# Sliding-window attention on one square of keys per head: own and older scores merged by a mask, values by differences

## The chip, the cores and the metric

The kernel runs on one core of a Trainium2 chip. A core has TensorE (PE: matmuls, and a separate stream of weight loads, PEld), VectorE (DVE), ScalarE (ACT), GpSimd (POOL) and SyncE (SP), which issues most of the transfers. The metric is the device time of one execution in microseconds (us); lower is better.

## The reference

One inference step of a trunk of two layers on 1024 prompt tokens and 8 single new tokens, in float32, with a width of 1024. Layer 0 is a gated linear recurrence with its MLP, layer 1 is sliding-window attention with its MLP. The change touches the attention of the prompt tokens only. There are 16 query heads, 4 key heads and 64 elements per head; the window is 128 tokens, and blocks are as long as the window.

```python
def sink_attention(q, k, v, dist, mask, sinks):
    s = jnp.einsum('...qkgd,...skd->...kgqs', q, k) * (HEAD_DIM ** -0.5)
    s = s - alibi_slopes()[:, :, None, None] * dist
    s = jnp.where(mask, s, NEG_INF)
    sink = sinks.reshape(N_KV, GROUP)[:, :, None, None]
    m = jnp.maximum(jnp.max(s, axis=-1, keepdims=True), sink)
    e = jnp.exp(s - m)
    p = e / (jnp.sum(e, axis=-1, keepdims=True) + jnp.exp(sink - m))
    return jnp.einsum('...kgqs,...skd->...qkgd', p, v)

def swa_prompt(...):                       # per block of 128 queries: keys of the block before and of its own
    ...
    dist = qi + BLOCK - si                 # qi: 0..127, si: 0..255
    mask = (dist >= 0) & (dist < WINDOW) & (key_pos >= 0)
    o = sink_attention(qb, with_prev(k), with_prev(v), dist, mask[:, None, None], sinks)
```

For a query `qi` of a block the window holds the own block's keys 0 to `qi` and the block before's keys `qi`+1 to 127. That is 128 keys of the 256: for each column of 128, either the own or the older key is inside the window, and never both.

## The kernel before, in words

The attention stage is one interleaved stream. It has 64 steps, `STEPS[j] = (t, b)`: `t` is one of 8 pairs of heads, `b` one of 8 blocks of 128 queries. Each step has three parts, and different steps' parts overlap by an order written out by hand (lines 1133 to 1175):

- `stage_a(j)` runs three steps ahead of the others (`AHEAD = 3`). For each of the two heads GpSimd makes the bias from the distances (line 953) and copies the sink's score into the last column of the probabilities' tile `se` (line 955). TensorE makes the scores of 128 queries by 256 keys, with the keys in a high and a low part (line 959), in one of two PSUM banks called "S". VectorE adds scores and bias and takes the row's extreme (line 963), ScalarE takes the exponential and its sum (line 966), VectorE the reciprocal (line 968), and GpSimd multiplies by it (line 971). Block 0 has no block before it and uses 128 keys.
- `stage_b(j)` transposes the probabilities on TensorE, four squares of 128 by 128 (two heads, two blocks of keys; two squares where b is 0), into the only PSUM bank "T" (line 981). One copy takes them to the tile `pt` in SBUF, by VectorE at even and by ScalarE at odd steps (line 986).
- `stage_c`, after every four steps, multiplies with the values (line 1003) into bank "O" and copies the result out (lines 1008 to 1013).

Between these parts TensorE does work that doesn't depend on them, called `fill`. Until step 52 (`J0`) this is the projection of the later queries and keys, 3 groups of three matmuls per step (line 886). From then on it is the output projection (line 245), whose weights are called `wo1`. Weights arrive as `raw`, ScalarE casts them to a high part `wh` (line 185), and VectorE makes the low part `wl` (line 186). The tuple `WHEN` says at which step each of the first output weights is fetched and split. Weights, values, probabilities and transposed probabilities share one pool of 12 working tiles, `W`; another pool is `A`.

Names in the rows: `bS`, `bT`, `bO`, `bP` are the PSUM banks of scores, transposes, value products and projections; `se` the probabilities, `den` their row sums, `fac` factors per token, `con` constants (distances, identity), `hh` and `hl` the high and low part of the layer's input.

Of the kernel before, what the change touches and what calls it, by code (L numbers as in the profile page):

```python
# [10 lines left out]
F32 = mybir.dt.float32  # L11
F32R = mybir.dt.float32r
AF = mybir.ActivationFunctionType
ALU = mybir.AluOpType
# [36 lines left out]
    VEC[_n] = (_off, _w)  # L51
    _off += _w
NVEC = _off
C_DIST, C_ID, C_BLK = 0, 256, 384
NCONST = 512

# [6 lines left out]
def trunk(ctx: ExitStack, tc: tile.TileContext, I, O):  # L65
# [37 lines left out]
    def W(s="w"):  # L103
        return wp.tile([P, T], F32, tag="W", name=nm(s))
# [29 lines left out]
        return c if isinstance(c, slice) else slice(c * CH, (c + 1) * CH)  # L134


    con = cp.tile([P, NCONST], F32, name="con")
    ones = cp.tile([P, P], F32, name="ones")
    pool.memset(ones, 1.0 / D)
    vec = cp.tile([P, NVEC], F32, name="vec")  # L140
# [1 line left out]
    act.dma_start(vec, I["vec"])  # L142
    ident = con[:, C_ID:C_ID + P]
    blk = con[:, C_BLK:C_BLK + P]
    distM = con[:, C_DIST:C_DIST + 256]

    def V(n, m=0):
        o, _ = VEC[n]
# [43 lines left out]
    def add_units(name, src, n, alloc=lambda j: W):  # L192
        for j in range(n):
            units.append((name, j, src[j], alloc(j)))
# [8 lines left out]
    for layer in range(2):  # L203
        add_units(f"up{layer}", I["w_up"][layer], 2 * NPAIR, lambda j: None)
        for b in range(4 * NCK):
            for j in range(2):
                units.append((f"dn{layer}", 2 * b + j, I[f"w_dn{layer}"][2 * b + j][:, 0:2 * P * len(CHUNKS[layer][b // 4])], None))
        add_units(f"ds{layer}", I[f"w_dn{layer}"][8 * NCK:], 2 * (NPAIR - NSP[layer]), lambda j: W)
        if layer == 0:
            for n, t in (("k", 0), ("q", 0), ("v", 0), ("v", 1), ("q", 1), ("q", 2), ("q", 3), ("k", 1),  # L210
                         ("q", 4), ("q", 5), ("q", 6), ("q", 7)):
                units.append((n, t, I["w_qkv"][{"q": 0, "k": 8, "v": 10}[n] + t], W))
            add_units("wo1", I["w_out1"], 8, lambda j: A if j in (2, 4) else W)
    index = {(n, j): k for k, (n, j, _, _) in enumerate(units)}
    nloaded = [0]

# [529 lines left out]
    def attention(hs):  # L746
# [141 lines left out]
                    yield  # L888
                due[2].append(lambda c=c, sx=take(c, o): evac(c, sx))

        v_tiles = [W("v") for _ in range(2)]
        vnew = tc.dram_tile([2, D], F32, name="vnew")

        def v_proj():
            w = [unit("v", 0, 1), unit("v", 1, 1)]

            def mms(o, sl):
                n = 0
                for k in range(M8):
                    wh, wl = w[k // 4]  # L900
                    xh, xl = hs[k]
                    ws = slice((k % 4) * 256, (k % 4) * 256 + 256)
                    for xt, wt in ((xh, wh), (xh, wl), (xl, wh)):
                        pe.matmul(o, lhsT=r_(xt[:, sl]), rhs=r_(wt[:, ws]), start=(n == 0), stop=(n == 3 * M8 - 1))  # L904
                        n += 1

            for b2 in range(NB // 2):
                ps = B("S")
                for j in range(2):
                    b = 2 * b2 + j  # L910
                    mms(ps[:, j * 256:j * 256 + 256], slice(b * P, b * P + P))
                for p, copy in enumerate((act.copy, dve.tensor_copy)):
                    copy(v_tiles[p][:, 2 * b2 * P:2 * b2 * P + 2 * P].rearrange("p (b d) -> p b d", b=2),
                         ps.rearrange("p (b q d) -> p b q d", b=2, q=2)[:, :, p, :])
                if b2 > 1:
                    stats0.pop()()
                if b2 == 3:
                    vo = S("vo")
                    act.copy(vo[:, :256], ps[:, 256:512])
                    sp.dma_start(O["v"], vo[:, :256])  # L920
            ps = B("T")
            mms(ps[:NS, :256], slice(SEQ, T))
            vo = S("vo")
            act.copy(vo[:NS, :256], ps[:NS, :256])
            sp.dma_start(vnew.rearrange("h (n j) -> (h n) j", n=4), vo[:NS, :256])

        bias2 = A("bias")
        ses = [W("se"), W("se")]
        ses = [x[:, h * 514:h * 514 + 514].rearrange("p (u k) -> p u k", u=2) for x in ses for h in range(2)]
        outs = {}  # L930
        ohl = {}
        srcs = [None] * M8
# [10 lines left out]
        def stage_a(j):  # L943
            t, b = STEPS[j]
            p, i = divmod(t, 4)
            se, dn, s = ses[j % 4], den[j % 4], B("S")
            hd = heads(t)
            k0 = max(b - 1, 0) * P
            n = P if b == 0 else 2 * P
            f = fac[t % 3]  # L950
            for u in range(2):
                o = (j % 2) * 512 + u * 256
                pool.tensor_scalar(bias2[:, o + 256 - n:o + 256], distM[:, 256 - n:256], f[:, 2 * NB + 2 * b + u:2 * NB + 2 * b + u + 1],  # L953
                                   0.25 * SLOPES[hd[u]], ALU.mult, ALU.mult)
            pool.tensor_copy(se[:, :, 256], nsink[:, hd[0]:hd[1] + 1:4])
            for u in range(2):
                for a, y in enumerate(kst[p][u]):
                  with after_values():
                    pe.matmul(s[:, u * 256:u * 256 + 256], lhsT=r_(qs[t][u][:, b * P:b * P + P]), rhs=r_(y[:, k0:k0 + 256]),  # L959
                              start=(a == 0), stop=(a == 1))  # L960
            for u in range(2):
                o = (j % 2) * 512 + u * 256 + 256
                dve.tensor_tensor_reduce(  # L963
                    se[:, u, 256 - n:256], s[:, u * 256:u * 256 + n], bias2[:, o - n:o],
                    scale=f[:, 2 * b + u:2 * b + u + 1], scalar=nsink[:, hd[u]:hd[u] + 1], op0=ALU.add, op1=ALU.min, accum_out=dn[:, u:u + 1])
                act.activation(se[:, u, 256 - n:257], se[:, u, 256 - n:257], AF.Exp, scale=-1.0,  # L966
                               bias=dn[:, u:u + 1], accum_out=dn[:, 2 + u:3 + u])
            dve.reciprocal(dn[:, 2:4], dn[:, 2:4])  # L968
            for u in range(2):
                e = se[:, u, 256 - n:256]  # L970
                pool.tensor_scalar(e, e, dn[:, 2 + u:3 + u], 0.0, ALU.mult, ALU.add)  # L971


        def stage_b(j):
            b = STEPS[j][1]
            se, pt = ses[j % 4], B("T")
            first = 1 if b == 0 else 0
            for h in range(first, 2):
                for u in range(2):
                  with after_values():  # L980
                    pe.transpose(pt[:, h * 256 + u * P:h * 256 + u * P + P], se[:, u, h * P:h * P + P], ident)  # L981
            if j % 2 == 0:
                live["pair"] = W("pt")
            pw = live["pair"][:, j % 2 * 512:j % 2 * 512 + 512]
            d = slice(256 * first, 512)
            (act.copy if j % 2 else dve.tensor_copy)(pw[:, d], pt[:, d])
            live["pt", j] = pw

        def stage_c(k):
            t, b0 = STEPS[4 * k]  # L990
            if b0 == 0 and t < 6:
                outs[t] = A("o")
            elif b0 == 0:
                srcs[t] = ohl[t] = (A("oh"), A("ol"))
            op, chain = B("O"), last["mm"]
            for b in range(b0 + 3, b0 - 1, -1):
                pw = live.pop(("pt", 4 * k + b - b0))
                first = 1 if b == 0 else 0
                for h in range(first, 2):
                    for u in range(2):  # L1000
                        at = (b - 1 + h) * P + 64 * u
                        with tc.issue_after(chain):
                            chain = pe.matmul(op[64 * u:64 * u + 64, (b - b0) * P:(b - b0) * P + P], lhsT=v_tiles[t // 4][:, at:at + 64],  # L1003
                                              rhs=pw[:, h * 256 + u * P:h * 256 + u * P + P], start=(h == first), stop=(h == 1)).ins
            last["values"] = chain
            dst = slice(b0 * P, b0 * P + 512)
            if t < 6:
                act.copy(outs[t][:, dst][:, 0:256], op[:, 0:256])
                dve.tensor_copy(outs[t][:, dst][:, 256:512], op[:, 256:512])
            else:  # L1010
                oh, ol = [x[:, dst] for x in ohl[t]]
                last["o"] = act.copy(r_(oh), op).ins
                dve.tensor_tensor(r_(ol), op, oh, ALU.subtract)
# [117 lines left out]
                next(fill, None)  # L1131

        NJ = 8 * NB
        WHEN = (44, 47, 49, 54, 60)
        AHEAD, T0, T1, TF, J0, JS = 3, 24, 5, 3.0, 52, 46
        take(T0)
        for j in range(AHEAD):
# [116 lines left out]
        with tc.issue_after(last["mm"]):  # L1254
            token_factors(ssq, rx[:, cs(c)])

    queue(sp, sp.dma_start, con, I["con"])
    cst = cp.tile([P, M8, 3, NS], F32, name="cst")
    pre = aux[:, 2 * P:2 * P + M8 * NS].rearrange("p (m n) -> p m n", m=M8)
    tap = S("tap")[:, :M8 * NS].rearrange("p (m n) -> p m n", m=M8)  # L1260
# [199 lines left out]
def _constants():  # L1460
# [1 line left out]
    qi = np.arange(P)[:, None]  # L1462
    si = np.arange(2 * P)[None, :]
    dist = qi + P - si
    con[:, C_DIST:C_DIST + 256] = np.where((dist >= 0) & (dist < P), dist, MASKED)
    con[:, C_ID:C_ID + P] = np.eye(P)
    h = np.arange(P) // 64
    con[:, C_BLK:C_BLK + P] = (h[:, None] == h[None, :]) / 64.0
# [113 lines left out]
```

## Time and profile before

| | |
|---|---|
| median of 3 runs | 1989.66 us (1988.62 to 1989.97) |
| the profiled execution, its own time | 1990.03 us |
| its span in the profile | 1988.1 us (1.93 us lie around it) |
| TensorE busy | 1980.2 us (100%) |
| VectorE, ScalarE, GpSimd busy | 1386.7, 1050.3, 376.2 us |
| TensorE clock granted | 1.00 |
| attention stage, about 1050 to 1256 us | TensorE 204.0 of 206 us, VectorE 141.3, ScalarE 139.1, GpSimd 137.6 |

The profile is one execution. Its groups give for each line and engine the count, the busy time, the mean duration of one instruction in nanoseconds, and the idle time of the engine just before them with what ended it. Matmuls overlap in the records, so a matmul's own duration is more than it adds to TensorE's time; the distance from start to start is what it adds. The chain of waits follows the execution back from its last instruction.

### The profile page before, as it was taken

To read this page: it belongs to the slowest core of one execution; us is meant where nothing else is said; L and a number is where in the kernel's file an instruction comes from. 1 tells how busy PE (TensorE), PEld (TensorE's weight loads), DVE (VectorE), ACT (ScalarE), POOL (GpSimd) and SP (SyncE) were. 2 spreads that over 40 slices of the span, in tenths; PEclk is the share of its full clock that TensorE was granted. 3 is DMA by queue.
4 is the path that set the end of the run, shared out by engine and by line. 5 is a ranking of instruction groups with operands and counts; after the bars stand their busy time and mean duration, and the time that the engine had idled before them with its cause. 6 is when DMAs were issued, how large, how long until landed. Compare 5 with 4: busy or idle time off the path is not lost.

```text
span 1988.1 us, 39291 instructions
## 1 busy us (share of the span) xinstructions
PE 1980.2 (100%) x15452; PEld 1950.6 (98%) x15452; DVE 1386.7 (70%) x2515; ACT 1050.3 (53%) x2049; POOL 376.2 (19%) x688
## 2 busy tenths in 40 slices
PE   9999999999999999999999999999999999999999
PEld 9999999999999999999999999999999999999999
DVE  7986638867666867767755767588666678776673
ACT  8786436444443655545445767465434346554551
POOL 2230100000001233312005767000000002332220
PEclk9999999999999999999999999999999999999999
DMA  5112322444436688777442324523434446877775
GB/s 173 52 44 64 130 99 72 147 147 139 155 129 223 198 224 228 207 186 198 123 126 70 89 72 148 179 78 124 162 127 155 139 150 202 239 210 187 205 193 132
DMA packets 110857, 294.41 MB, mean 148 GB/s; under 512 B 18488, under 2 KB 43328, under 8 KB 110672
## 3 DMA queue, kind: packets, MB, share of 16 engines
q1 hardware_dynamic: 53712, 125.82, 20.7%
q0 software_dynamic: 29024, 97.85, 19.1%
q10 hardware_dynamic: 27936, 68.23, 9.4%
q8 instruction: 121, 1.98, 0.4%
q14 instruction: 64, 0.52, 0.1%
HBM read 170.97 MB, written 108.19 MB: 140 GB/s over the span
## 4 chain that ended last, share of the span: by engine, by line
PE 96%; DVE 1%; DMA 1%; ACT 1%; issue 1%; POOL 0%; ACTq 0%; SPq 0%; DVEq 0%; POOLq 0%
PE bD L557 61%; PE bP L245 11%; PE bS L245 7%; PE bP L886 4%; PE bO L245 3%; PE bT L245 3%; PE bS L959 1%; PE bO L1003 1%; PE bT L981 1%; PE bS L904 1%; DMA tl<-hsum 1%; DVE tl L431 0%; DVE op L425 0%; PE bN L829 0%; PE bN L773 0%
## 5 line engine op out<-in xcount | busy, mean ns | idle before, releaser
L557 PE MATMUL bD<-op,op 128*128 128x258 f32 x5544 | 678.7, 284 | 0.0
L557 PEld LDWEIGHTS bD<-op,op 128*128 128x128 f32 x5544 | 671.2, 190 | 5.0 <-ACT ho L692 4.5
L557 PE MATMUL bD<-tl,op 128*128 128x258 f32 x4704 | 580.4, 284 | 0.5 <-DVE ho L696 0.3
L557 PEld LDWEIGHTS bD<-tl,op 128*128 128x128 f32 x4704 | 570.7, 189 | 7.6 <-ACT ho L692 5.7
L571 POOL DMA_DIRECT2D tl<-hsum x196 | 113.2, 678 | 940.5 <-ACT op L424 414.9
L425 DVE TENSOR_TENSOR op<-ws,op 128x384 fp32r<-128x384 f32 (+2 forms) x288 | 172.2, 606 | 94.1 <-ACT op L424 94.0
L692 ACT COPY he<-bD 128x516 f32<-128x516 f32 x144 | 84.9, 590 | 275.1 <-PE bD L557 275.0
L424 ACT CAST op<-ws 128x384 fp32r<-128x384 f32 (+2 forms) x288 | 158.5, 555 | 109.5 <-PE bD L557 70.9
L692 ACT COPY ho<-bD 128x516 f32<-128x516 f32 x144 | 84.9, 590 | 192.2 <-PE bD L557 192.1
L431 DVE TENSOR_TENSOR tl<-tl 128x516 fp32r<-128x516 f32 x196 | 129.9, 690 | 76.1 <-ACT tl L430 76.0
L424 ACT CAST op<-raw 128x384 fp32r<-128x384 f32 (+2 forms) x216 | 116.9, 556 | 44.0 <-PE bD L557 19.3
L425 DVE TENSOR_TENSOR op<-raw,op 128x384 fp32r<-128x384 f32 (+2 forms) x216 | 127.6, 604 | 6.4 <-ACT op L424 2.4
L700 DVE TENSOR_TENSOR ho<-bD,ho 128x516 f32<-128x516 f32 x72 | 49.9, 693 | 106.5 <-PE bD L557 106.5
L430 ACT CAST tl<-tl 128x516 fp32r<-128x516 f32 x196 | 116.5, 628 | 7.9 <-DMA tl<-hsum 6.7
L963 DVE CUSTOM_DVE_ANT_0 se<-bS,bias,nsink 128x256 f32<-128x256 f32 (+1 forms) x128 | 63.6, 523 | 21.6 <-PE bS L959 15.2
L186 DVE TENSOR_TENSOR wl<-raw,wh 128x1024 fp32r<-128x1024 f32 (+1 forms) x54 | 63.5, 1184 | 20.2 <-ACT wh L185 12.4
L696 DVE TENSOR_TENSOR ho<-bD,ho 128x516 f32<-128x516 f32 x72 | 49.7, 690 | 39.6 <-ACT ho L692 38.8
L966 ACT ACTIVATE se<-se,den 128x257 f32<-128x257 f32 (+1 forms) x128 | 62.8, 492 | 26.7 <-DVE den L963 21.2
L953 POOL TENSOR_SCALAR bias<-con,fac 128x256 f32<-128x256 f32 (+1 forms) x128 | 63.2, 498 | 34.6 <-DVE den L963 24.1
L971 POOL TENSOR_SCALAR se<-se,den 128x256 f32<-128x256 f32 (+1 forms) x128 | 65.5, 525 | 14.0 <-DVE den L968 9.6
L711 POOL DMA_DIRECT2D spill<-ho x32 | 28.6, 892 | 208.6 <-DVE ho L700 206.6
L886 PE MATMUL bP<-hh,wh 128*128 128x384 f32 (+2 forms) x192 | 67.2, 350 | 0.0
(399 smaller groups left out, 3709.0 us busy)
## 6 DMA issues: line engine op xcount, KB each, us to landing
tl<-hsum POOLq DMA_DIRECT2D x196, 258.0 KB, 6.3
raw<-w_up SPq DMA_DIRECT2D x64, 512.0 KB, 4.4
raw<-w_dn SPq DMA_DIRECT2D x72, 384.0 KB, 6.1
spill<-he POOLq DMA_DIRECT2D x32, 516.0 KB, 9.9
spill<-ho POOLq DMA_DIRECT2D x32, 516.0 KB, 7.0
hsum<-ho ACTq DMA_DIRECT2D x28, 516.0 KB, 2.7
hsum<-he ACTq DMA_DIRECT2D x28, 516.0 KB, 2.7
hsum<-ts ACTq DMA_DIRECT2D x28, 516.0 KB, 3.0
```

The source lines that it names most:

```text
L186: eng.tensor_tensor(r_(lo[:, sl]), raw[:, sl], hi[:, sl], ALU.subtract)
L245: last["mm"] = pe.matmul(o, lhsT=r_(wt[:, col(k):col(k) + P]), rhs=r_(xt[:, cs(c)]), start=(k == 0 and a == 0), stop=(k == nk - 1 and a == ...
L424: act.copy(r_(t[:, 0:n]), src)
L425: dve.tensor_tensor(r_(t[:, n:2 * n]), src, t[:, 0:n], ALU.subtract)
L430: act.copy(r_(hi), lo)
L431: dve.tensor_tensor(r_(lo), lo, hi, ALU.subtract)
L557: ins = pe.matmul(d[:, 512 * b:512 * b + QT], lhsT=r_(wt[:, j * P:j * P + P]), rhs=r_(xt[:, QT * b:QT * b + QT]), start=first and j == 0 a ...
L571: pool.dma_start(t[:, n:2 * n], src)
L692: last["copy"] = act.copy(t, f).ins
L886: last["mm"] = pe.matmul(o, lhsT=r_(wt[:, k * P:k * P + P]), rhs=r_(xt[:, sl]), start=(k == 0 and a == 0), stop=(k == M8 - 1 and a == 2)).ins
L963: dve.tensor_tensor_reduce(se[:, u, 256 - n:256], s[:, u * 256:u * 256 + n], bias2[:, o - n:o], scale=f[:, 2 * b + u:2 * b + u + 1], scala ...
L971: pool.tensor_scalar(e, e, dn[:, 2 + u:3 + u], 0.0, ALU.mult, ALU.add)
```

## The change

With b > 0 the scores of 256 keys are still made in the same bank. Then ScalarE copies the own block's 128 columns of both heads to `se`, and VectorE overwrites, where a constant mask of the pair (query, key) says so, with the older block's score: a predicated copy. Bias, score sum, exponential, sum and normalisation then run on 128 columns instead of 256. One square per head is transposed instead of two; ScalarE copies it out at every step, and VectorE writes a second copy multiplied by the transposed mask, which holds the older keys' part alone.

The values follow from: own·V(b) + older·V(b−1) = (own + older)·V(b) + older·(V(b−1) − V(b)). The differences `dv` are made once, by GpSimd, two instructions of 128 by 896. The value products keep their number and shape, four per step (two where b is 0).

The masks are two more blocks of 256 columns in the constants in DRAM, brought by one more transfer on SP into the second half of the bias tile, whose halves had held biases of 256 keys. Two tiles `dv` are added to the pool `W` and one of the two tiles of `se` goes. The tuple `WHEN` has a sixth entry, 62, and the sixth output weight takes its tile from the other pool, `A`.

```diff
-            add_units("wo1", I["w_out1"], 8, lambda j: A if j in (2, 4) else W)
+            add_units("wo1", I["w_out1"], 8, lambda j: A if j in (2, 4, 5) else W)
...
+            for x in v_tiles:
+                dv.append(W("dv"))
+                pool.tensor_tensor(dv[-1][:, 0:SEQ - P], x[:, 0:SEQ - P], x[:, P:SEQ], ALU.subtract)
...
         bias2 = A("bias")
-        ses = [W("se"), W("se")]
-        ses = [x[:, h * 514:h * 514 + 514].rearrange("p (u k) -> p u k", u=2) for x in ses for h in range(2)]
+        sp.dma_start(bias2[:, 512:1024], I["con"][:, C_OWN:])
+        older, older_t = bias2[:, 512:768].bitcast(mybir.dt.int32), bias2[:, 768:1024]
+        ses = W("se")
+        ses = [ses[:, h * 258:h * 258 + 258].rearrange("p (u k) -> p u k", u=2) for h in range(4)]
...
+            bias = [bias2[:, (j % 2) * 256 + u * P:(j % 2) * 256 + u * P + P] for u in range(2)]
             for u in range(2):
-                o = (j % 2) * 512 + u * 256
-                pool.tensor_scalar(bias2[:, o + 256 - n:o + 256], distM[:, 256 - n:256], f[:, 2 * NB + 2 * b + u:2 * NB + 2 * b + u + 1],
+                pool.tensor_scalar(bias[u], dist if b else dist0, f[:, 2 * NB + 2 * b + u:2 * NB + 2 * b + u + 1],
                                    0.25 * SLOPES[hd[u]], ALU.mult, ALU.mult)
...
+            s = s.rearrange("p (u h k) -> p u h k", u=2, h=2)
+            if b:
+                act.copy(se[:, :, 0:P], s[:, :, 1, :])
+                dve.copy_predicated(se[:, :, 0:P], older.rearrange("p (u k) -> p u k", u=2), s[:, :, 0, :])
             for u in range(2):
-                o = (j % 2) * 512 + u * 256 + 256
+                e = se[:, u, 0:P]
                 dve.tensor_tensor_reduce(
-                    se[:, u, 256 - n:256], s[:, u * 256:u * 256 + n], bias2[:, o - n:o],
+                    e, e if b else s[:, u, 0, :], bias[u],
                     scale=f[:, 2 * b + u:2 * b + u + 1], scalar=nsink[:, hd[u]:hd[u] + 1], op0=ALU.add, op1=ALU.min, accum_out=dn[:, u:u + 1])
-                act.activation(se[:, u, 256 - n:257], se[:, u, 256 - n:257], AF.Exp, scale=-1.0,
-                               bias=dn[:, u:u + 1], accum_out=dn[:, 2 + u:3 + u])
+                act.activation(se[:, u, :], se[:, u, :], AF.Exp, scale=-1.0, bias=dn[:, u:u + 1], accum_out=dn[:, 2 + u:3 + u])
...
-            first = 1 if b == 0 else 0
-            for h in range(first, 2):
-                for u in range(2):
-                  with after_values():
-                    pe.transpose(pt[:, h * 256 + u * P:h * 256 + u * P + P], se[:, u, h * P:h * P + P], ident)
+            for u in range(2):
+                with after_values():
+                    pe.transpose(pt[:, u * P:u * P + P], se[:, u, 0:P], ident)
...
-            d = slice(256 * first, 512)
-            (act.copy if j % 2 else dve.tensor_copy)(pw[:, d], pt[:, d])
+            act.copy(pw[:, 0:256], pt[:, 0:256])
+            if b:
+                dve.tensor_tensor(pw[:, 256:512], pt[:, 0:256], older_t, ALU.mult)
...
-                for h in range(first, 2):
+                for h, vb in enumerate(((v_tiles, b), (dv, b - 1)) if b else ((v_tiles, b),)):
...
-        WHEN = (44, 47, 49, 54, 60)
+        WHEN = (44, 47, 49, 54, 60, 62)
```

The order of the instructions on TensorE, at one step of the second pair of heads. Before:

```order
L959 MATMUL bS_12425<-kl_11388,q_11921 128x256
...
L981 MATMUL bT_12443<-con,se_11337 128x128 x4
L886 MATMUL bP_12390<-hh_10743,wh_12021 128x384
L886 MATMUL bP_12390<-hl_10744,wh_12021 128x384
L886 MATMUL bP_12390<-hh_10743,wl_12022 128x384
...
L959 MATMUL bS_12455<-kh_11385,q_11920 128x256
```

The same place on TensorE after the change:

```order
L963 MATMUL bS_12439<-kl_11388,q_11925 128x256
...
L986 MATMUL bT_12459<-con,se_11337 128x128 x2
L886 MATMUL bP_12403<-hh_10743,wh_12025 128x384
L886 MATMUL bP_12403<-hl_10744,wh_12025 128x384
L886 MATMUL bP_12403<-hh_10743,wl_12026 128x384
...
L963 MATMUL bS_12470<-kh_11385,q_11924 128x256
```

Two transposes are left at the place of four; the projection and the scores around them stand as they did.

The order on VectorE at the same place (`ISA` is the score sum, with the reading of its extreme behind it). Before:

```order
L963 ISA se_11337,den_11327<-bS_12425,bias_11335,nsink,fac_11330 128x256
L963 ISA den_11327 128x1
...
L968 RECIPROCAL den_11327<-den_11327 128x2
L963 ISA se_11337,den_11328<-bS_12455,bias_11335,nsink,fac_11330 128x256
L963 ISA den_11328 128x1
...
L986 COPY pt_12476<-bT_12473 128x256
L968 RECIPROCAL den_11328<-den_11328 128x2
```

VectorE after the change:

```order
L968 COPY_PREDICATED se_11337<-bias_11335,bS_12439 128x2x128
L992 TENSOR_TENSOR pt_12430<-bT_12459,bias_11335 128x256
L971 ISA se_11337,den_11327<-se_11337,bias_11335,nsink,fac_11330 128x128
L971 ISA den_11327 128x1
...
L968 COPY_PREDICATED se_11337<-bias_11335,bS_12470 128x2x128
L971 ISA se_11337,den_11328<-se_11337,bias_11335,nsink,fac_11330 128x128
L971 ISA den_11328 128x1
L975 RECIPROCAL den_11327<-den_11327 128x2
```

The predicated copy stands ahead of the score sums, and the multiplication of the step three back stands between them. Both new instructions wait for ScalarE's copy of the same bank.

The order on ScalarE at the end of the stage, where `wh` is a cast of an output weight and `y`, `sq`, `x` belong to the output projection. Before:

```order
L986 COPY pt_14800<-bT_14814 128x512
L385 DMA spill_2510<-y_14837 128x344
L296 ACTIVATE sq_14840<-y_14837 128x344
L387 ACTIVATE x_14835<-y_14837,vec 128x344
...
L387 ACTIVATE x_14844<-y_14846,vec 128x344
L185 CAST wh_14855<-raw_14713 128x1024
L185 CAST wh_14861<-raw_14853 128x1024
L1012 CAST oh_14738<-bO_14882 128x512
```

After the change:

```order
L990 COPY pt_14792<-bT_14832 128x256
L185 CAST wh_14852<-raw_14777 128x1024
L385 DMA spill_2510<-y_14823 128x344
L296 ACTIVATE sq_14826<-y_14823 128x344
L387 ACTIVATE x_14675<-y_14823,vec 128x344
L990 COPY pt_14866<-bT_14863 128x256
L385 DMA spill_2510<-y_14837 128x344
L296 ACTIVATE sq_14840<-y_14837 128x344
L387 ACTIVATE x_14677<-y_14837,vec 128x344
L185 CAST wh_14921<-raw_14850 128x1024
```

A cast that stood behind the last copies of transposes now stands between them.

More of the change, by code (lines that the diff above doesn't have):

```diff
@@ L53 @@
 NVEC = _off
-C_DIST, C_ID, C_BLK = 0, 256, 384
-NCONST = 512
+C_DIST, C_ID, C_BLK, C_OWN, C_PREV = 0, 256, 384, 512, 768
+NCONST = 1024
 LRU = [(s[0], int(s[1])) for s in (
@@ L134, in cs @@
         return c if isinstance(c, slice) else slice(c * CH, (c + 1) * CH)
-    con = cp.tile([P, NCONST], F32, name="con")
+    con = cp.tile([P, C_OWN], F32, name="con")
     ones = cp.tile([P, P], F32, name="ones")
@@ L144, in trunk @@
     blk = con[:, C_BLK:C_BLK + P]
-    distM = con[:, C_DIST:C_DIST + 256]
+    dist, dist0 = (con[:, C_DIST + k * P:C_DIST + k * P + P] for k in range(2))
     def V(n, m=0):
@@ L889, in proj_steps @@
                 due[2].append(lambda c=c, sx=take(c, o): evac(c, sx))
-        v_tiles = [W("v") for _ in range(2)]
+        v_tiles, dv = [W("v") for _ in range(2)], []
         vnew = tc.dram_tile([2, D], F32, name="vnew")
@@ L948, in stage_a @@
             k0 = max(b - 1, 0) * P
-            n = P if b == 0 else 2 * P
             f = fac[t % 3]
+            bias = [bias2[:, (j % 2) * 256 + u * P:(j % 2) * 256 + u * P + P] for u in range(2)]
             for u in range(2):
-                o = (j % 2) * 512 + u * 256
-                pool.tensor_scalar(bias2[:, o + 256 - n:o + 256], distM[:, 256 - n:256], f[:, 2 * NB + 2 * b + u:2 * NB + 2 * b + u + 1],
+                pool.tensor_scalar(bias[u], dist if b else dist0, f[:, 2 * NB + 2 * b + u:2 * NB + 2 * b + u + 1],
                                    0.25 * SLOPES[hd[u]], ALU.mult, ALU.mult)
-            pool.tensor_copy(se[:, :, 256], nsink[:, hd[0]:hd[1] + 1:4])
+            pool.tensor_copy(se[:, :, P], nsink[:, hd[0]:hd[1] + 1:4])
             for u in range(2):
@@ L960, in stage_a @@
                               start=(a == 0), stop=(a == 1))
+            s = s.rearrange("p (u h k) -> p u h k", u=2, h=2)
+            if b:
+                act.copy(se[:, :, 0:P], s[:, :, 1, :])
+                dve.copy_predicated(se[:, :, 0:P], older.rearrange("p (u k) -> p u k", u=2), s[:, :, 0, :])
             for u in range(2):
-                o = (j % 2) * 512 + u * 256 + 256
+                e = se[:, u, 0:P]
                 dve.tensor_tensor_reduce(
-                    se[:, u, 256 - n:256], s[:, u * 256:u * 256 + n], bias2[:, o - n:o],
+                    e, e if b else s[:, u, 0, :], bias[u],
                     scale=f[:, 2 * b + u:2 * b + u + 1], scalar=nsink[:, hd[u]:hd[u] + 1], op0=ALU.add, op1=ALU.min, accum_out=dn[:, u:u + 1])
-                act.activation(se[:, u, 256 - n:257], se[:, u, 256 - n:257], AF.Exp, scale=-1.0,
-                               bias=dn[:, u:u + 1], accum_out=dn[:, 2 + u:3 + u])
+                act.activation(se[:, u, :], se[:, u, :], AF.Exp, scale=-1.0, bias=dn[:, u:u + 1], accum_out=dn[:, 2 + u:3 + u])
             dve.reciprocal(dn[:, 2:4], dn[:, 2:4])
             for u in range(2):
-                e = se[:, u, 256 - n:256]
+                e = se[:, u, 0:P]
                 pool.tensor_scalar(e, e, dn[:, 2 + u:3 + u], 0.0, ALU.mult, ALU.add)
@@ L997, in stage_c @@
                 pw = live.pop(("pt", 4 * k + b - b0))
-                first = 1 if b == 0 else 0
-                for h in range(first, 2):
+                for h, vb in enumerate(((v_tiles, b), (dv, b - 1)) if b else ((v_tiles, b),)):
                     for u in range(2):
-                        at = (b - 1 + h) * P + 64 * u
+                        at = vb[1] * P + 64 * u
                         with tc.issue_after(chain):
-                            chain = pe.matmul(op[64 * u:64 * u + 64, (b - b0) * P:(b - b0) * P + P], lhsT=v_tiles[t // 4][:, at:at + 64],
-                                              rhs=pw[:, h * 256 + u * P:h * 256 + u * P + P], start=(h == first), stop=(h == 1)).ins
+                            chain = pe.matmul(op[64 * u:64 * u + 64, (b - b0) * P:(b - b0) * P + P], lhsT=vb[0][t // 4][:, at:at + 64],
+                                              rhs=pw[:, h * 256 + u * P:h * 256 + u * P + P], start=(h == 0), stop=(h == 1 or b == 0)).ins
             last["values"] = chain
@@ L1255, in factor @@
             token_factors(ssq, rx[:, cs(c)])
-    queue(sp, sp.dma_start, con, I["con"])
+    queue(sp, sp.dma_start, con, I["con"][:, :C_OWN])
     cst = cp.tile([P, M8, 3, NS], F32, name="cst")
@@ L1464, in _constants @@
     dist = qi + P - si
-    con[:, C_DIST:C_DIST + 256] = np.where((dist >= 0) & (dist < P), dist, MASKED)
+    own = np.arange(P)[None, :] <= qi
+    con[:, C_DIST:C_DIST + P] = np.where(own, dist[:, P:], dist[:, :P])
+    con[:, C_DIST + P:C_DIST + 2 * P] = np.where(own, dist[:, P:], MASKED)
+    con[:, C_OWN:C_PREV] = np.tile(~own, 2)
+    con[:, C_PREV:] = np.tile(~own.T, 2)
     con[:, C_ID:C_ID + P] = np.eye(P)
```

## The prediction

> **What bounds the kernel now.** I read the page first (span, busy shares, chain), then the busy time by stretch of the attention stage, then the groups by form inside it, and last single instructions in order of time.
>
> ```profile
> span 1988.1 us, 39291 instructions
> PE 1980.2 (100%) x15452; PEld 1950.6 (98%) x15452; DVE 1386.7 (70%) x2515; ACT 1050.3 (53%) x2049; POOL 376.2 (19%) x688
> PE 96%; DVE 1%; DMA 1%; ACT 1%; issue 1%; POOL 0%; ACTq 0%; SPq 0%; DVEq 0%; POOLq 0%
> ```
>
> TensorE is busy all the time and carries 96% of the chain that ended last. So an instruction taken from TensorE shortens the kernel, as long as the others still deliver in time. The edits touch only the attention stage, about 1050 to 1256 us of the span. These are its stretches (busy us of PE, weight load, DVE, ACT, POOL; then clock, DMA share, GB/s):
>
> ```profile
> 1062.00:1197.00 135.00, 134.95 (x1199) 126.39 (x1198) 92.20 (x322) 93.14 (x292) 98.00 (x233) 1.00 0.30 77
> 1197.00:1217.00 20.00, 19.71 (x190) 18.20 (x188) 19.64 (x56) 18.02 (x51) 16.06 (x30) 1.00 0.41 108
> 1217.00:1238.00 21.00, 20.88 (x174) 19.70 (x174) 15.27 (x51) 12.80 (x41) 17.74 (x41) 1.00 0.47 161
> 1238.00:1256.00 18.00, 16.46 (x138) 15.22 (x133) 9.02 (x17) 9.56 (x18) 0.32 (x1) 1.00 0.74 242
> ```
>
> In the long first stretch TensorE lacks 0.05 us of 135 while the three side engines are near 70% busy: all their waits are covered. In the second (the output weights are split there too) VectorE is as full as TensorE, 19.64 against 19.71. In the last, TensorE idles 1.54 us. The granted clock is 1.00 throughout.
>
> **The change part by part.** The prices, by form, within the stage (count, then busy us and mean ns of one, then idle time before it):
>
> ```profile
> L981 PE MATMUL bT<-con,se 128*128 128x128 f32 x240 | 37.2, 273 | 0.2
> L963 DVE CUSTOM_DVE_ANT_0 se<-bS,bias,nsink 128x256 f32<-128x256 f32 x112 | 57.6, 539 | 19.6 <-PE bS L959 13.3 <-POOL se L971 4.9 <-POOL bias L953 0.6
> L963 DVE CUSTOM_DVE_ANT_0 se<-bS,bias,nsink 128x128 f32<-128x128 f32 x16 | 6.0, 408 | 2.0 <-PE bS L959 1.9
> L966 ACT ACTIVATE se<-se,den 128x257 f32<-128x257 f32 x112 | 56.4, 506 | 20.2 <-DVE den L963 14.6 <-DVE den L968 2.9 <-POOL se L971 2.6
> L966 ACT ACTIVATE se<-se,den 128x129 f32<-128x129 f32 x16 | 6.3, 397 | 6.6 <-DVE den L963 6.6
> L971 POOL TENSOR_SCALAR se<-se,den 128x256 f32<-128x256 f32 x112 | 59.7, 547 | 13.4 <-DVE den L968 9.6 <-ACT fac L791 2.6
> L971 POOL TENSOR_SCALAR se<-se,den 128x128 f32<-128x128 f32 x16 | 5.8, 374 | 0.6
> L953 POOL TENSOR_SCALAR bias<-con,fac 128x256 f32<-128x256 f32 x110 | 54.6, 499 | 32.2 <-DVE den L963 24.1 <-DVE den L968 4.9
> L986 ACT COPY pt<-bT 128x512 f32<-128x512 f32 x32 | 18.3, 572 | 5.2 <-PE bT L981 5.2
> L986 DVE COPY pt<-bT 128x512 f32<-128x512 f32 x24 | 16.5, 686 | 1.5 <-PE bT L981 1.5
> L1008 ACT COPY o<-bO 128x256 f32<-128x256 f32 x12 | 4.5, 372 | 13.0 <-PE bO L1003 13.0
> L1009 DVE COPY o<-bO 128x256 f32<-128x256 f32 x12 | 5.1, 422 | 9.1 <-ACT o L1008 9.1
> L1013 DVE TENSOR_TENSOR ol<-bO,oh 128x512 fp32r<-128x512 f32 x4 | 2.7, 687 | 2.7 <-ACT oh L1012 2.7
> L384 DVE TENSOR_TENSOR y<-bP,x 128x344 f32<-128x344 f32 x4 | 2.0, 514 | 1.5 <-PE bP L245 1.5
> ```
>
> *Transposes.* The 240 are 4 in each of 56 steps and 2 in each of 8 with block 0; 112 go. Scores and value products keep number and shape. The mean of 273 ns overlaps neighbours and is no price; the starts are:
>
> ```profile
> 1126.70 0.60 PE L981 MATMUL bT<-con,se 128*128 128x128 f32 x4
> 1129.18 0.60 PE L981 MATMUL bT<-con,se 128*128 128x128 f32 x4
> 1129.54 0.42 PE L886 MATMUL bP<-hh,wh 128*128 128x384 f32 x1
> 1129.80 0.34 PE L886 MATMUL bP<-hl,wh 128*128 128x384 f32 x1
> ...
> 1178.46 0.38 PE L981 MATMUL bT<-con,se 128*128 128x128 f32 x2
> 1178.59 0.37 PE L886 MATMUL bP<-hh,wh 128*128 128x264 f32 x1
> 1178.80 0.29 PE L886 MATMUL bP<-hl,wh 128*128 128x264 f32 x1
> ```
>
> From the start of four transposes to the start of the second projection matmul is 0.62 us; a projection matmul of 384 columns advances by some 0.175, so four cost 0.445. For two, 0.34 less 0.12 (264 columns) is 0.22. Two saved are worth 0.22, and the chain of waits in order of time shows the same 0.44 for four where they lie on it:
>
> ```profile
> 1214.06 0.44 PE bT L981 x4
> ```
>
> 56 × 0.22 = **−12.3 us**, all on the engine that sets the end.
>
> *Work per step with b > 0 on the side engines.* VectorE before: two score sums and half of the 512-wide copies, 2×539 + 686/2 = 1421 ns. After: two sums at 128 columns (2×408), a predicated copy of 256 elements out of PSUM, and the multiplication of 256 elements. The trace has no predicated copy: I take 422, the plain copy of that size from PSUM; the lower end is the same, the upper 686, as if it cost like 512 elements. The multiplication, from 514 at 344 columns and 687 at 512, comes to 424. Sum 1662: +0.24 us, or +0.50 at the upper end. ScalarE: 2×506 + 572/2 = 1298 becomes 2×397 + 372 + 372 = 1538, +0.24. GpSimd: 2×(547+499) = 2092 becomes at most 4×374 = 1496, −0.60.
>
> The first stretch holds 173 of the 240 transposes, so 46 steps (40 with b > 0); the second 7, the third 8. First: VectorE 92.2+10 = 102 to 112, ScalarE 103, GpSimd 74, in 135 − 40×0.22 = 126. Nobody is full; I take +0.5 for waits (bounds 0 and 3). Second: VectorE 19.64 + 7×0.24 = 21.3 in 20 − 1.5 = 18.5, so TensorE waits: **+2.8** (0 if the spare of the third stretch, where VectorE would have 17 of 19.3, takes it up; 4.6 with the dear copy).
>
> *The sixth output weight earlier.* In the last stretch TensorE waits for a cast:
>
> ```profile
> 1248.56 0.94 ACT wh L185
> PE bP L245 <- ACT wh L185: 1.4, 1, 1.4
> ```
>
> With the entry 62 this cast stands ahead, between the last copies of transposes, and ScalarE has 9.56 busy of 18 there: **−1.4** (bounds −1.5 and +0.9, if the cast delays the last transposes' copy by its own 0.94).
>
> *Differences of the values.* Two subtractions of 896 columns on GpSimd, at best 1.2 us (896/256 × the 547 less a fixed part of some 200), at worst twice that for two inputs. They stand ahead of the first bias, and GpSimd has idled ten microseconds there:
>
> ```profile
> 1052.42 1.05 POOL L953 TENSOR_SCALAR bias<-con,fac 128x256 f32<-128x256 f32 x2 [10.38 <-DVE den L963]
> ```
>
> Cost 0; without this cover up to 5 us, once. *The masks:* 256 KB more by SP, issued behind the copies of the keys, before the first mask is wanted at 1052. A transfer twice as large lands in 4.4 us:
>
> ```profile
> raw<-w_up SPq DMA_DIRECT2D x64, 512.0 KB, 4.4
> ...
> 1013.24 2.45 SPq L868 DMA_DIRECT2D kh<-hi  x4
> ```
>
> Cost 0. Queued behind it on SP are the next weight's transfers, 20 us and more ahead of their use. One working tile more is bound (two for differences, one fewer for probabilities); a weight cast could wait for it, with no stall in sight: 0, at most one cast.
>
> *Sum:* −12.3 + 2.8 + 0.5 − 1.4 = −10.4 on the profiled execution's 1990.03, so 1979.6; the median lies 0.37 lower. I say **1979.5**.
>
> **A new wait, weighed.** The multiplication reads the same PSUM bank as ScalarE's copy, and by the order it waits for ScalarE; behind it on VectorE stand the next score sums. There is one bank for transposes. Its round was 0.60 + 0.57 to 0.69; it becomes 0.38 + 0.37 + 0.42 = 1.17, in a turn of 2.48 − 0.22 = 2.26 us. 1.09 us remain for waits of either copy in its queue. The Trainium skill, "PSUM — Partial Sum Buffer", section "PSUM bank collisions raise a hardware error", says that two engines must not touch one bank and quadrant at once, and that the compiler's scheduler orders them; the serial wait seen in the order agrees. Read side by side, without the serial wait, the round would be 0.8 and the sum the same.
>
> **The rivals.**
>
> (a) As summed, 1979.5: 0.55.
>
> (b) No new waits at all, because the stretches lend each other lead: 1990.0 − 12.3 − 1.4 = 1976: 0.12.
>
> (c) The predicated copy is dear (0.69 or more). VectorE gets 0.50 per step: 23.1 of 18.5 in the second stretch and 112 of 126 in the first, +4.6 and +2: 1984. For it speaks that it has three operands, against it that nothing here shows it: 0.17.
>
> (d) GpSimd slows down. It did where VectorE ran a tensor operation with two SBUF inputs:
>
> ```profile
> 1128.83 0.94 POOL L971 TENSOR_SCALAR se<-se,den 128x256 f32<-128x256 f32 x2
> 1200.58 2.52 POOL L971 TENSOR_SCALAR se<-se,den 128x256 f32<-128x256 f32 x2
> ...
> 1200.46 1.22 DVE L186 TENSOR_TENSOR wl<-raw,wh 128x1024 fp32r<-128x1024 f32 x1
> 1201.68 1.07 DVE L277 TENSOR_TENSOR ol<-o,oh 128x680 fp32r<-128x680 f32 x1
> ```
>
> The pair took 2.52 instead of 0.94 over some 2.1 us of these: 0.75 lost per us shared. The new score sums read the copied scores and the bias, both in SBUF, where before one input was PSUM. Shared all through, 2×0.41×0.75 = 0.61 per step go, and GpSimd is back at 2.1 of 2.74 us: not full, but the probabilities come 0.3 later in the 7 tight steps, +2: 1981.5. The Trainium skill, "GPSIMD Engine Reference", sections "1. Specifications" and "8. Key points", names it: GpSimd shares its SBUF interfaces with VectorE and contends with instructions that have two SBUF inputs. The 2.52 agrees. Chance 0.06.
>
> (e) Slower: the one bank for transposes. If the copy and the multiplication together wait more than 1.09 us per step in their queues (a 0.94 cast or a 1.2 us split ahead of either), TensorE waits at the next transposes. It wins nothing from 0.22 of waiting beyond this, that is from 1.31. At 1.5 us, 56 × 0.41 = 23 against −12.3 and −1.4: 2000. Against it: before, the same bank's copy waited in the same queues and the 240 transposes lost 0.2 us in all (first row of the prices): 0.06.
>
> (f) The gain is not TensorE's to have: another engine sets the step and the time stays, 1988. The side engines' 70% speak against it: 0.04.
>
> **How the numbers follow.** What differs by under 0.2% (4 us) can't be told from no change here. Cases (a), (b), (d) and most of (c) lie below 1985.7: faster 0.86. (f) and the dear end of (c) give same 0.08, (e) slower 0.06. The range runs from (b) with half a microsecond to spare, 1975.5, to beyond (c), 1986.5; what lies outside is (e), (f) and the ends.
>
> **What would show it.** Transposes: 128 records, two at a start-to-start of 0.22, and TensorE's busy time in the stage down by 12. The predicated copy: its mean near 422, the multiplication near 424. VectorE full and TensorE with idle time ahead of transposes near 1197 to 1217. The wait on the cast near 1249 gone. GpSimd's pair of normalisations near 0.75 and not 1.3. I am wrong if TensorE's idle time before the transposes or the scores adds to more than 6 us, or if a predicated copy costs 0.8.

## The result, and the profile after

The changed kernel takes 1979.28 us (median of 6 runs, 1978.68 to 1980.06) against 1989.66 (median of 6 runs, 1988.62 to 1989.97): 0.9949 of the time before, 95% interval 0.9936 to 0.9962. The forecast was 1979.5. The profiled execution took 1979.64, with a span of 1977.9.

The page's head, engine shares and chain of the kernel after:

```profile
span 1977.9 us, 39178 instructions
PE 1969.2 (100%) x15340; PEld 1937.4 (98%) x15340; DVE 1397.7 (71%) x2595; ACT 1057.9 (53%) x2137; POOL 363.9 (18%) x690
PE 95%; DVE 2%; DMA 1%; ACT 1%; issue 1%; POOL 0%; ACTq 0%; SPq 0%; DVEq 0%; POOLq 0%
```

TensorE is still busy all the time. It lost 112 instructions and 11.0 us; VectorE and ScalarE gained 11.0 and 7.6, GpSimd lost 12.3. VectorE's share of the chain rose from 1% to 2%: the first sign of a new wait. The same stretches by the clock as before (the work in them has moved forward by up to ten microseconds):

```profile
1062.00:1197.00 135.00, 133.16 (x1151) 122.06 (x1150) 104.14 (x391) 102.58 (x367) 89.52 (x240) 1.00 0.31 81
1197.00:1217.00 20.00, 20.00 (x192) 18.84 (x191) 19.72 (x70) 18.43 (x63) 15.96 (x35) 1.00 0.57 166
1217.00:1238.00 21.00, 20.61 (x172) 18.80 (x171) 15.85 (x54) 15.19 (x51) 11.13 (x29) 1.00 0.40 134
```

The first stretch, which lacked 0.05 us of TensorE's time before, now lacks 1.84. The second, where VectorE is as full as it was (19.72 of 20), lacks nothing. Nor do the steps that lay in it before: they now run between about 1192 and 1212 us, where TensorE has 20.00 of 20 us busy. The groups by form inside the stage say what the new instructions cost and who waits:

```profile
L986 PE MATMUL bT<-con,se 128*128 128x128 f32 x128 | 24.8, 275 | 1.9 <-DVE pt L992 1.6
L971 DVE CUSTOM_DVE_ANT_0 se<-se,bias,nsink 128x128 f32<-128x128 f32 x112 | 43.4, 417 | 3.7
L968 DVE COPY_PREDICATED se<-bias,bS 128x256 f32<-128x256 int32 x56 | 25.1, 448 | 8.1 <-ACT se L967 7.0
L992 DVE TENSOR_TENSOR pt<-bT,bias 128x256 f32<-128x256 f32 x56 | 23.4, 418 | 2.2 <-ACT pt L990 1.8
L967 ACT COPY se<-bS 128x256 f32<-128x256 f32 x56 | 20.6, 369 | 11.4 <-PE bS L963 10.5 <-POOL bias L957 0.6
L990 ACT COPY pt<-bT 128x256 f32<-128x256 f32 x64 | 23.8, 371 | 12.0 <-PE bT L986 10.8
L974 ACT ACTIVATE se<-se,den 128x129 f32<-128x129 f32 x128 | 50.6, 399 | 9.5 <-DVE den L971 8.9
L978 POOL TENSOR_SCALAR se<-se,den 128x128 f32<-128x128 f32 x128 | 49.7, 401 | 3.2 <-DVE den L975 1.5
```

TensorE's idle time ahead of the transposes went from 0.2 to 1.9 us, and the profile puts 1.6 of that down to the multiplication of line 992, at six places. The starts tell more. At 15 of the 64 steps the transposes start 0.15 to 0.17 us after a multiplication has ended, whatever else runs then; all of the 1.9 us lies there, and their probabilities had been normalised at least 1.35 us earlier. Idle time is not all that these places cost, since the modelled end of the matmul before covers a part. Measured from the start of that matmul, less the usual distance behind a matmul of its kind, the 15 are 3.7 us late in all; in the kernel before, transposes that start right behind a copy of the bank were 0.5 us late. The longest of these waits, in order of time on TensorE, ScalarE and VectorE:

```profile
1122.35 0.38 PE L986 MATMUL bT<-con,se 128*128 128x128 f32 x2
1122.93 0.36 ACT L990 COPY pt<-bT 128x256 f32<-128x256 f32 x1
...
1124.01 0.52 DVE L786 TENSOR_TENSOR x<-x,hi 128x344 fp32r<-128x344 f32 x1 [0.84 <-POOL aux L864]
1124.45 0.41 DVE L971 CUSTOM_DVE_ANT_0 se<-bS,bias,nsink 128x128 f32<-128x128 f32 x1
...
1124.78 0.42 DVE L992 TENSOR_TENSOR pt<-bT,bias 128x256 f32<-128x256 f32 x1
1125.34 0.43 PE L986 MATMUL bT<-con,se 128*128 128x128 f32 x2 [0.56 <-DVE pt L992]
```

ScalarE has copied the bank at 1123.29. The multiplication, which needs the same bank, stands on VectorE behind the splitting of a key chunk, which itself waits 0.84 us for GpSimd, and behind a score sum. So it starts at 1124.78, and the next transposes, which must write that bank, come 0.56 us late. Here VectorE sat waiting while the bank was held. Four of the other places, at 0.18 to 0.21 us each, look like this one:

```profile
1087.52 0.46 DVE L968 COPY_PREDICATED se<-bias,bS 128x256 f32<-128x256 int32 x1 [0.25 <-ACT se L967]
...
1088.79 0.42 DVE L992 TENSOR_TENSOR pt<-bT,bias 128x256 f32<-128x256 f32 x1
1089.36 0.41 PE L986 MATMUL bT<-con,se 128*128 128x128 f32 x2 [0.18 <-DVE pt L992]
```

The predicated copy waits for ScalarE's copy of the scores, two score sums follow it, and only then comes the multiplication. VectorE mostly works here; the bank is held because the multiplication is not next in its order.

### The profile page after: what moved, and what is told of

It reads as the page before. It is cut to its first block, busy times and chain, and to the rows that moved or that the text cites. A ratio compares the mean times of both kernels' runs of the same rounds, so it can differ in the third digit from the quotient of the medians.

```text
span 1977.9 us, 39178 instructions
## 1 busy us (share of the span) xinstructions
PE 1969.2 (100%) x15340; PEld 1937.4 (98%) x15340; DVE 1397.7 (71%) x2595; ACT 1057.9 (53%) x2137; POOL 363.9 (18%) x690
## 4 chain that ended last, share of the span: by engine, by line
PE 95%; DVE 2%; DMA 1%; ACT 1%; issue 1%; POOL 0%; ACTq 0%; SPq 0%; DVEq 0%; POOLq 0%
PE bD L557 61%; PE bP L245 12%; PE bS L245 7%; PE bP L886 4%; PE bT L245 3%; PE bO L245 3%; PE bS L963 1%; PE bO L1008 1%; DMA tl<-hsum 1%; PE bS L904 1%; PE bT L986 1%; DVE tl L431 0%; DVE se L971 0%; DVE op L425 0%; PE bN L829 0%
## 5 line engine op out<-in xcount | busy, mean ns | idle before, releaser
L957 POOL TENSOR_SCALAR bias<-con,fac 128x128 f32<-128x128 f32 x128 | 61.5, 487 | 47.6 <-DVE den L971 40.8
L694 DVE TENSOR_TENSOR he<-bD,he 128x516 f32<-128x516 f32 x72 | 49.7, 691 | 21.0 <-PE bD L557 15.5
L886 PE MATMUL bP<-hh,wl 128*128 128x384 f32 (+2 forms) x192 | 62.1, 323 | 0.0
L296 ACT ACTIVATE sq<-y 128x344 f32<-128x344 f32 x48 | 23.6, 492 | 71.4 <-DVE y L384 66.0
```

What stands on the lines that cost most here:

```text
L886: last["mm"] = pe.matmul(o, lhsT=r_(wt[:, k * P:k * P + P]), rhs=r_(xt[:, sl]), start=(k == 0 and a == 0), stop=(k == M8 - 1 and a == 2)).ins
L957: pool.tensor_scalar(bias[u], dist if b else dist0, f[:, 2 * NB + 2 * b + u:2 * NB + 2 * b + u + 1], 0.25 * SLOPES[hd[u]], ALU.mult, ALU.mult)
```

## Experiments

All were timed in five or more rounds beside the kernel before. "Against before" is the difference from that kernel's median beside which the run was made (1989.49 in the first four, 1989.32 in the last four). The theory at the outset: TensorE gains 0.22 us per pair of transposes and 1.4 at the weight cast, and pays waits; the traces point to the bank as the place of these. An edit also changes the order in which the side engines run the steps' instructions. In again VectorE's sequence in the stage is that of the changed kernel; with the sixth weight it differs at a few places, and in the other experiments at dozens. So a difference between two of those kernels is not the edited line's alone, and the starts in the traces are read beside it.

**again**: the changed kernel, for comparison.

> The changed kernel once more, beside the next three on the same chip: 1979.3 us, within 0.7. Both theories below take its TensorE idle time ahead of the transposes (1.9 us in the first trace) as the thing to explain.

Measured 1979.20 (1978.51 to 1979.41), ratio 0.9949 (0.9936 to 0.9961), −10.3.

**mult_sbuf**: the multiplication reads the copy.

```diff
-                dve.tensor_tensor(pw[:, 256:512], pt[:, 0:256], older_t, ALU.mult)
+                dve.tensor_tensor(pw[:, 256:512], pw[:, 0:256], older_t, ALU.mult)
```

> The masked multiplication reads ScalarE's copy in SBUF instead of the bank of the transposes. Theory 'bank': the short waits of TensorE ahead of the transposes come from the one bank, held until VectorE gets to the multiplication. Then they go (1.9 us of idle time to under 0.5) and the time falls by 1.5 to 2.5, to about 1977.3. Rival 'late probabilities': the waits come from probabilities that are ready late; then the idle time stays and so does the time, 1979.3. Second rival 'shared SBUF': the multiplication now has two SBUF inputs, and GpSimd's normalisation (401 ns here) slows to over 450.

Measured 1977.30 (1976.91 to 1978.22), ratio 0.9940 (0.9928 to 0.9953), −12.2: 1.9 less than the changed kernel, with no run in common. Its groups:

```profile
L986 PE MATMUL bT<-con,se 128*128 128x128 f32 x128 | 24.6, 273 | 0.1
L992 DVE TENSOR_TENSOR pt<-pt,bias 128x256 f32<-128x256 f32 x56 | 24.4, 437 | 1.1 <-ACT pt L990 0.9
L978 POOL TENSOR_SCALAR se<-se,den 128x128 f32<-128x128 f32 x128 | 55.3, 444 | 3.7 <-DVE den L975 2.8
```

The idle time ahead of the transposes fell from 1.9 to 0.1, and counted by starts the lateness behind a reader of the bank from 3.7 to 0.4. The multiplication comes no earlier: it starts 0.56 us after ScalarE's copy ends, as a mean of the 56, against 0.51 in the changed kernel. So the bank was the cause, not late probabilities. The time fell by less than that lateness; one part of the difference is new idle time of TensorE, 0.8 us at line 829, where it waits for ScalarE. GpSimd's normalisation slowed from 401 to 444 ns, just short of the 450 named; no matmul waited for it. Of the kernels here that use the older keys' probabilities this is the fastest.

**no_sixth** and **before_sixth**: the sixth output weight's earlier fetch taken from the changed kernel, and added alone to the kernel before.

```diff
-            add_units("wo1", I["w_out1"], 8, lambda j: A if j in (2, 4, 5) else W)
+            add_units("wo1", I["w_out1"], 8, lambda j: A if j in (2, 4) else W)
...
-        WHEN = (44, 47, 49, 54, 60, 62)
+        WHEN = (44, 47, 49, 54, 60)
```

> The changed kernel with the five entries of WHEN and the pools of before. Theory 'cast': TensorE waits 1.4 us for the cast near the end of the stage again, against 0.3 with the sixth entry: 1980.4 (+1.1). Rival 'late again': the wait has only another place, and the time is the same within 0.5.

> The kernel before with the sixth entry of WHEN and its pool alone. Theory 'cast': the 1.4 us wait near 1249 goes and nothing else changes: 1988.1. Rival: in the kernel before, the earlier cast and split fall into its crowded stretch (VectorE 19.6 of 20 us) or the wait finds another place: 1989.5 to 1990.5. The run before_two lost that wait without the entry, which speaks for the rival.

no_sixth: 1980.98 (1980.51 to 1981.51), ratio 0.9958 (0.9946 to 0.9971), 1.8 more than the changed kernel. before_sixth: 1988.00 (1987.72 to 1988.61), ratio 0.9994 (0.9984 to 1.0003), −1.3; its interval reaches 1, so the gain alone is not clear of the measurement, though no run of the two kernels is in common and the size is as expected. The two waits that no_sixth has and the changed kernel lacks:

```profile
PE bP L245 <- ACT wh L185: 1.1, 1, 1.1
PE bT L245 <- DVE pt L992: 0.4, 1, 0.4
```

The wait for the cast is back with 1.1 us, and another of 0.4 with it. In before_sixth no wait of TensorE on a cast is left in the stage.

**before_two**: the kernel before with 112 transposes left out. It leaves out the older keys' probabilities, so it serves only to price the transposes.

```diff
-            for h in range(first, 2):
+            for h in range(1, 2):
                 for u in range(2):
                   with after_values():
                     pe.transpose(pt[:, h * 256 + u * P:h * 256 + u * P + P], se[:, u, h * P:h * P + P], ident)
...
-            d = slice(256 * first, 512)
+            d = slice(256, 512)
...
-                                              rhs=pw[:, h * 256 + u * P:h * 256 + u * P + P], start=(h == first), stop=(h == 1)).ins
+                                              rhs=pw[:, 256 + u * P:256 + u * P + P], start=(h == first), stop=(h == 1)).ins
```

> The kernel before with the older block's two transposes and half of the copy left out (the value products read the own block's square twice); softmax stays on 256 keys and nothing is added. It prices the 112 transposes alone. Theory '0.22 a pair': 1989.7 - 12.3 = 1977.4. Rival '0.18 a pair' (which the sum of the change, read without its waits, would need): 1979.6.

Measured 1976.29 (1975.13 to 1976.76), ratio 0.9933 (0.9920 to 0.9947), −13.2, nearer to the dearer price. All that TensorE still waits for in the stage, over 0.2 us:

```profile
PE bP L245 <- ACT oh L1012: 0.3, 1, 0.3
```

The 1.4 us wait for the cast has gone here too, though the weight is fetched as before. So −13.2 is about −11.9 for the transposes, with the shorter copies, and −1.3 for that wait: 0.21 a pair. The traces agree with the split: from the first scores to the last value product this kernel takes 187.2 us, and before_sixth, which lacks the wait too, 199.0. What made the wait go was not tested; the copies are shorter and the order around the end has shifted.

**four_again**: the changed kernel with four transposes again.

```diff
+            if b:
+                for u in range(2):
+                    with after_values():
+                        pe.transpose(pt[:, 256 + u * P:256 + u * P + P], se[:, u, 0:P], ident)
```

> The changed kernel with two more transposes per step, of the same squares, into the bank's unused half, never copied. Theory '0.22 a pair, plus waits of the bank': 1979.2 + 12.4 less up to 1 for waits that the longer turn covers: 1991, so slower than before. Rival 'the price is smaller beside the new work': 1987 or less.

Measured 1990.24 (1989.58 to 1991.49), ratio 1.0004 (0.9995 to 1.0013), +0.9: with all the rest of the change in place, the kernel is back at the time before. TensorE's waits in its stage:

```profile
PE bT L986 <- POOL se L959: 0.3, 1, 0.3
```

The profile puts this one down to GpSimd, but the transposes in question start 0.15 us after a multiplication has ended and 6.6 us after their probabilities were ready: it is the bank again. Against the changed kernel the time is +11.2, or 0.20 a pair. The longer turn also makes the bank cheaper: 15 pairs of transposes still start right behind a multiplication, but they are 1.6 us late in all by their starts, where it was 3.7. With these 2.1 us the pair comes to 0.24, so 0.22 lies between the two.

Against before_sixth it is +2.2: what the other work costs beside four transposes. TensorE's idle time in the stage does not show it (195.45 of 196 us busy, against 195.42). The starts show some of it: from the first scores to the last value product the same matmuls take 200.9 us against 199.0, and the lateness behind a reader of the bank, 1.6 against 0.5, is 1.1 of these 1.9; the rest of them is open. Another piece lies ahead of the stage, where TensorE waits longer at line 773; the row of before and that of after:

```profile
1022.30 0.84 PE L773 MATMUL bN<-sq,con 128*128 128x344 f32 x2 [0.22 <-ACT sq L766]
```

```profile
1022.05 0.85 PE L773 MATMUL bN<-sq,con 128*128 128x344 f32 x2 [0.82 <-ACT sq L766]
```

That is 0.6 us more idle time, and it is lost in full: the 300 matmuls ahead of the first scores take 38.4 us in every kernel here without the change and 39.0 in every one with it. Its cause was not tried. In the same kernels two casts of weights stand 20 us later; before and after:

```profile
1018.35 1.05 ACT L185 CAST wh<-raw 128x1024 fp32r<-128x1024 f32 x1
...
1020.53 1.06 ACT L185 CAST wh<-raw 128x1024 fp32r<-128x1024 f32 x1
```

```profile
1038.44 2.00 ACT L185 CAST wh<-raw 128x1024 fp32r<-128x1024 f32 x2
```

**twice_copy** and **twice_sbuf**: the predicated copy issued twice, in the changed kernel and in mult_sbuf.

```diff
-                dve.copy_predicated(se[:, :, 0:P], older.rearrange("p (u k) -> p u k", u=2), s[:, :, 0, :])
+                for _ in range(2):
+                    dve.copy_predicated(se[:, :, 0:P], older.rearrange("p (u k) -> p u k", u=2), s[:, :, 0, :])
```

> The changed kernel with the predicated copy issued twice: VectorE gets 0.45 us more in each of 56 steps, 25 us in all, as if the copy cost 0.9. Theory 'bank': the multiplication comes later and holds the bank of the transposes; TensorE's waits ahead of the transposes grow from 1.9 to 5 to 10 us: 1983 to 1988. Rival 'lent lead': VectorE had 31 us idle of 135 in the first stretch and TensorE sees nothing of it: 1980.

> The same doubling with the multiplication out of SBUF. Theory 'bank': the bank no longer waits for VectorE, so most of the 25 us are covered: 1978 to 1980.5. Rival 'VectorE is full': the loss is the same as in the run before, +4 to +9 on 1977.3.

twice_copy: 1980.67 (1980.12 to 1981.03), ratio 0.9956 (0.9942 to 0.9970), −8.7, so 1.6 more than the changed kernel. twice_sbuf: 1980.70 (1980.48 to 1981.07), ratio 0.9956 (0.9943 to 0.9969), −8.6, so 3.6 more than mult_sbuf. The first stretch and the waits in twice_copy:

```profile
1062.00:1197.00 135.00, 134.01 (x1157) 123.13 (x1155) 117.07 (x434) 103.59 (x372) 89.19 (x239) 1.00 0.32 83
...
PE bT L987 <- DVE den L976: 1.1, 3, 0.7
PE bO L1009 <- ACT pt L991: 0.5, 1, 0.5
PE bS L963 <- ACT se L967: 0.4, 1, 0.4
PE bT L987 <- DVE pt L993: 0.3, 1, 0.3
```

VectorE has 117 of 135 us busy, and TensorE lacks less there than without the doubling (0.99 against 1.84). The list names the reciprocal of line 976 for 1.1 us, but the starts point to the bank; the longest of these places:

```profile
1106.93 0.42 DVE L993 TENSOR_TENSOR pt<-bT,bias 128x256 f32<-128x256 f32 x1
...
1107.49 0.41 PE L987 MATMUL bT<-con,se 128*128 128x128 f32 x2 [0.72 <-DVE den L976]
```

Here too the transposes start 0.15 us after the multiplication has ended, and their probabilities had been ready for 5.9 us. So it is at 20 steps, which hold all of the 1.6 us of idle time ahead of the transposes. The theory 'bank' had this idle time grow from 1.9 to 5 to 10 us; it stayed, at 1.6, and the time came nearer to the rival's 1980. The new idle time of TensorE is 0.9 us, at the value products and the scores, both waiting for ScalarE's copies; the rest of the 1.6 us lost is not placed. The two kernels don't differ by the doubling alone, since the multiplications and score sums stand in another sequence on VectorE, so this is no clean test of the bank. It is one of VectorE's load: 25 us more cost 1.6 and 3.6 us.

In twice_sbuf the time lies just above the range of the theory 'bank' (1978 to 1980.5) and the loss just below that of its rival (4 to 9). With the bank free, the transposes come to wait for normalised probabilities (0.9 us, and they start as these are ready), and the value products for the multiplication's result (0.7): the chain of a step, not the bank. So the freed bank, worth 1.9 us without the doubling, gains nothing with it: 1980.70 against 1980.67.

## Why the prediction was right, and where it was off

**Transposes, −12.3.** Right. 0.22 a pair from starts; 0.21 by before_two, and 0.20 to 0.24 by four_again. The saving lies on the engine that sets the end, so nearly all of it came through.

**Prices of the new instructions.** The predicated copy took 448 ns; forecast 422, with bounds of 422 and 686. The multiplication took 418 (424), the score sum 417 (408), ScalarE's copies 369 and 371 (372). VectorE has 2×417 + 448 + 418 = 1700 ns per step where 1662 was forecast. GpSimd's saving was smaller than forecast: "at most 4×374" took the normalisation's price for the bias too, whose own row of that size stood at 507 before. It is 475 after, so GpSimd has 2×(401+475) = 1752 ns per step and not 1496, and 89.5 us in the first stretch where 74 was forecast; that cost nothing. The rows of the bias, before and after:

```profile
L953 POOL TENSOR_SCALAR bias<-con,fac 128x128 f32<-128x128 f32 x14 | 7.0, 507 | 2.0 <-DVE fac L796 1.1
```

```profile
L957 POOL TENSOR_SCALAR bias<-con,fac 128x128 f32<-128x128 f32 x124 | 58.1, 475 | 47.2 <-DVE den L971 40.8 <-DVE fac L796 2.2 <-DVE den L975 0.4
```

Rival (c), the dear copy, is out; and its price was too high as well, since twice_copy made the copy cost 0.9 and lost 1.6, not the 4.5 by which (c) lay above the forecast at 0.69.

**Waits, +2.8 in the second stretch and +0.5 in the first.** The sum's weak step. The second stretch lacks nothing and the first lacks 1.84. The reckoning by capacity, VectorE's work against a stretch's length, found the wrong place: with VectorE at 19.72 of 20 us TensorE stood at 20.00. What made TensorE wait was the order on VectorE while one bank was held: the mechanism of rival (e), which was given a threshold of 1.09 us of queue waits in every step. It acted at 15 steps and not in all, wherever other work or a wait stood ahead of the multiplication: the 0.84 us for GpSimd at the worst, a predicated copy that waited for ScalarE and two score sums at four more. The trace shows 1.9 us of idle time there and 3.7 by starts, and mult_sbuf gives 1.9 of the time back. So the size of the term, +3.3, came out near and its reason did not, and that is luck. The 0.6 us ahead of the stage had no term.

The sum itself gives 1979.6 for the profiled execution and 1979.3 for the median, since that lies 0.37 lower; 1979.5 stands between the two.

**The sixth weight, −1.4.** Right: −1.3 alone, and 1.8 when taken out of the changed kernel.

**Differences and masks, 0.** No matmul waits for either, as forecast. "A weight cast could wait" for the one working tile less, put at 0, did come about: two casts stand 20 us later. Whether the 0.6 us ahead of the stage hang on that is open. The two subtractions took 2.1 us each, near the dear end of the estimate, and GpSimd afterwards still waited 6.4 us for work:

```profile
1037.69 4.22 POOL L923 TENSOR_TENSOR dv<-v 128x896 f32<-128x896 f32 x2 [9.20 <-ACT v L913]
...
1052.67 0.83 POOL L957 TENSOR_SCALAR bias<-con,fac 128x128 f32<-128x128 f32 x2 [6.36 <-DVE den L971]
```

**Rival (d), GpSimd slowed by VectorE.** Small. The normalisation took 401 ns against 374 for the same size before, so a pair is 0.80 us: near the 0.75 without sharing, far from 1.3. No matmul of the changed kernel waits for it. The profile names it for 1.3 us of the weight loads' idle time at three places:

```profile
PEld bT L986 <- POOL se L978: 1.3, 3, 0.6
```

But these loads belong to transposes that the bank made late; their probabilities had been ready for 1.35 to 4.2 us.

The sum in parts that were run, each against the next: the sixth weight −1.3, the side work with the old transposes +2.2, the transposes −11.2; together −10.3. The forecast's parts were −1.4, +3.3 and −12.3. The −11.2 hold the 2.1 us by starts that the bank costs more with the shorter turn.

## What to carry to other kernels

Where one engine is busy all the time, the price of its instructions by the distance of their starts is a good forecast of what leaving them out gives. What the other engines get in exchange has to be judged by what they hold while they are late as well as by their load: here one bank with two readers in turn cost 1.9 us at a load of 77%, and 25 us more load cost 1.6 to 3.6. When a second reader can take its input from the first one's output, the bank is free earlier: that gave 1.9 us here, and nothing once VectorE had the 25 us more. And when a wait is put down to an engine, compare the start with the ends of all that the instruction needs: three lists here named GpSimd or a reciprocal where the constant 0.15 us behind the multiplication showed the bank.

## What the runs showed of the hardware

In these runs, sharing between VectorE and GpSimd depends on the instruction, not only on its inputs lying in SBUF. GpSimd's 128x128 normalisation took 375 ns where nothing ran on VectorE beside it (17 of 128 in the changed kernel), and 374 and 382 where it ran longest beside the predicated copy or the multiplication out of PSUM. Beside the score sum with both inputs in SBUF it took 420 (22 of them), and in mult_sbuf, beside the multiplication out of SBUF, 618 (20 of them), though score sum and multiplication are about equally long. Over all 128 that makes 401 and 444 ns. Beside the wide splits it is plain; in the kernel after, on GpSimd and on VectorE:

```profile
1199.37 1.25 POOL L978 TENSOR_SCALAR se<-se,den 128x128 f32<-128x128 f32 x2
1209.63 0.72 POOL L978 TENSOR_SCALAR se<-se,den 128x128 f32<-128x128 f32 x2
...
1199.95 0.51 DVE L277 TENSOR_TENSOR ol<-o,oh 128x344 fp32r<-128x344 f32 x1
```

The pair took 1.25 us beside two score sums and a split, and 0.72 beside the multiplication out of PSUM and the predicated copy. The rule of the Trainium skill, "GPSIMD Engine Reference", section "1. Specifications", that VectorE's instructions with two SBUF inputs contend with GpSimd, holds here in direction; its size in these runs reaches from 12% (420 against 375) to 74% (1.25 against 0.72).
